# One tile at a time in the first pass of a two-layer decoder trunk: work order on four engines, and a share of the weight splitting moved to GpSimd

## The chip, the core and the metric

The kernel runs on one core of one Trainium2 chip. Its engines are named as the profile names them: PE (TensorE, matrix products; PEld is its weight loads), DVE (VectorE), ACT (ScalarE), POOL (GpSimd) and SP (SyncE, which here only issues DMA transfers). Each engine works through its own queue in order and waits on semaphores for the others. The metric is the device time of one execution in microseconds (us), median of several runs.

## The reference

Two decoder layers over 256 tokens of width 1024. Each layer is a token mixer (dilated window attention in layer 0, gated linear attention in layer 1) and a gated feed-forward part. Ahead of each, the tokens are normed and then scaled and shifted by vectors that come from a conditioning vector c:

```python
mod = jax.nn.silu(c) @ w_ada[i] + b_ada[i]
sh1, sc1, g1, sh2, sc2, g2 = jnp.split(mod, 6, axis=-1)
h = rmsnorm(x, norm_mix[i]) * (1.0 + sc1) + sh1
y = dilated_mixture(h, w_in_a[j], w_out_a[j], rel_bias)   # begins with qkv = h @ w_in_a[j]
```

This case is about the first product of layer 0 only: h @ w_in_a for the first heads, for which sc1 and sh1 have to be computed first. Everything is float32.

## The kernel before

**Three products for one.** A float32 product is made of rounded parts: a weight tile is cast to a reduced format ("whi"), and the rest is kept beside it ("wlo", raw less whi). The normed tokens have the same two parts, hhi and hlo. PE then does hhi with whi (part 0), hlo with whi (part 1) and hhi with wlo (part 2).

**The first pass** runs over eight tiles kt of 128 rows of the model's width. Each needs two transfers on SP's queue: `ada_raw` (or `early_x`, a borrowed room), 128 x 2048 columns of w_ada, of which the second half gives sc1 and the first half sh1, and `raw`, 1920 columns of w_in_a. For tiles 0 and 1 each transfer is cut in two. The 1920 columns are two halves in the code's words, `pieces`: columns 0 to 768 (half 0) and 768 to 1920 (half 1). The work of one tile is:

- `dots` (L421, L160): on DVE two products of 1024 columns with silu(c), each summed to one column; behind each, ACT makes the entry of `mod`, at L168 the scale, at L170 the shift.
- `scaled` (L430): xr on DVE, the tokens times rstd and the scale.
- `shifted` (L434): hhi on ACT, xr plus the shift, cast.
- `rest_of` (L438): hlo on DVE, xr plus the shift less hhi.
- `cast` (L446): whi of one half, on ACT, 768 or 1152 columns.
- `low` (L451): wlo of one half, on DVE.
- `products` (L683): on PE one part for some of three pieces. Piece 0 (six matmuls of 256 columns, from half 0) and piece 2 (six, from the last 768 columns of half 1) are queries and keys of two head pairs; piece 1 (two matmuls of 384 columns, L690, from the first 384 columns of half 1) is the values.

**What sets the order.** A scheduler places the instructions, but `behind` (L120) ties each to one that stands ahead of it on the same engine, and so the order on DVE, ACT and PE in this pass is the one written out. From tile 2 on it is shifted by a tile: ACT casts both halves of tile kt-1 and then makes the two `mod` entries and hhi of tile kt; DVE does the dots of kt, low half 0 of kt-1, xr of kt, low half 1 of kt-1, hlo of kt. On PE a tile's part 2 stands in among the parts 0 and 1 of the next one. GpSimd has no part in it; it copies the bias table (L368) up to 18.9 us and issues bias transfers (L382, L383) from 47.9 us.

**Buffers.** `raw` and `ada_raw` share four buffers, so a transfer of a later tile is issued when the dots or the lows of an earlier one are done with theirs. whi and wlo have three buffers each. Behind the pass come the evacuation of its results from PSUM (L601 to L609), the casts and lows of the next weights (L189, L193) and the next matmuls (L658).

Of the kernel before, what the change touches and what calls it, by code (L numbers as in the profile page):

```python
# [11 lines left out]
F32 = mybir.dt.float32  # L12
# [3 lines left out]
AF = mybir.ActivationFunctionType  # L16
ALU = mybir.AluOpType

P = 128
D = 1024  # L20
T = 256
KT = D // P
# [18 lines left out]
C_NMIX = C_BADA + 96  # L41
C_NFFN = C_NMIX + 16
# [15 lines left out]
def trunk(ctx: ExitStack, tc: tile.TileContext, I, out):  # L58
    nc = tc.nc
# [12 lines left out]
    def bank(name="ps", tag=None):  # L72
        tag = tag or next(cycle)
        return psum.tile([P, 512], F32, tag=tag, name=name, bufs={"p": 2, "s": 4, "t": 2}[tag])
# [21 lines left out]
    def col(at):  # L96
        return small[:, at : at + 1]
# [11 lines left out]
    one_b = const.tile([P, 32], F32, name="one_b")  # L109

    def scale_terms(sub):
        at = C_BADA + 24 * sub + 8
        b = small[:, at : at + 96].rearrange("p (l k) -> p l k", l=2)[:, :, 0:KT]
        g = small[:, (C_NMIX, C_NFFN)[sub] :][:, 0:16].rearrange("p (l k) -> p l k", l=2)
        return nc.vector.scalar_tensor_tensor(one_b[:, 16 * sub : 16 * sub + 16].rearrange("p (l k) -> p l k", l=2), b, 1.0, g,
                                              op0=ALU.add, op1=ALU.mult)


    @contextmanager
    def behind(*those):  # L120

        with ExitStack() as st:
            for i in those:
                st.enter_context(tc.issue_after(i.ins))
            yield
# [27 lines left out]
        return modulation(raw, l, n)  # L153

    def modulation(raw, l, n, order=(0, 1), between=None):
        for s in order:
            piece, kt = ADA_ORDER[2 * n + s]
            dot = tmp.tile([P, 1], F32, tag="dot", name="dot", bufs=4)
            w = raw[:, D * s : D * s + D]
            last_dot[0] = nc.vector.tensor_tensor_reduce(  # L160
                w, w, c_bc, op0=ALU.mult, op1=ALU.add, scale=1.0, scalar=0.0, accum_out=dot,
            )
            m = state.tile([P, 1], F32, tag=f"mod{l}{piece}{kt}", name="mod")
            b = col(C_BADA + 48 * l + 8 * piece + kt)
            if piece in (1, 4):
                g = col((C_NMIX if piece == 1 else C_NFFN) + 8 * l + kt)
                b1 = (16 if piece == 4 else 0) + 8 * l + kt
                last = nc.scalar.activation(m, dot, AF.Identity, scale=g, bias=one_b[:, b1 : b1 + 1])  # L168
            else:
                last = nc.scalar.activation(m, dot, AF.Identity, bias=b)  # L170
            mod[l, piece, kt] = m
            if between and s == order[0]:
                between(last)
        return last


# [227 lines left out]
    w0, h, xr, raw0 = [], [], [None] * KT, []  # L404
    pieces = (slice(0, 6 * P), slice(6 * P, 15 * P))
    on_act = [norm_ops[1]]
# [2 lines left out]

    def load(kt):  # L410
        chunk = rooms[0] if kt % 2 else wraw.tile([P, 2048], F32, tag="raw", name="ada_raw")
        for c in (slice(D, 2 * D), slice(0, D)) if kt < 2 else (slice(0, 2 * D),):
            nc.sync.dma_start(chunk[:, c], I["w_ada"][0, kt][:, c])
        raw = wraw.tile([P, 2048], F32, tag="raw", name="raw")
        for c in pieces if kt < 2 else (slice(0, 15 * P),):
            last_load[0] = nc.sync.dma_start(raw[:, c], I["w0"][kt][:, c])
        raw0.append(raw)
        w0.append([wspl.tile([P, 2048], F32R, tag=f"w{part}", name=f"w{part}") for part in ("hi", "lo")])
        return chunk

    def dots(kt, between=None):  # L421
        chunk = load(kt)
        with behind(on_dve[0], on_act[0]):
            on_act[0] = modulation(chunk, 0, kt, (1, 0), between)
        on_dve[0] = last_dot[0]

    def scaled(kt):
        xr[kt] = tmp.tile([P, T], F32, tag="xr", name="xr")
        with behind(on_dve[0]):
            on_dve[0] = nc.vector.scalar_tensor_tensor(xr[kt], x[kt], mod[0, 1, kt][:, 0:1], r, op0=ALU.mult, op1=ALU.mult)  # L430

    def shifted(kt):
        with behind(on_act[0]):
            on_act[0] = nc.scalar.activation(h_hi[kt][:, :], xr[kt], AF.Identity, bias=mod[0, 0, kt][:, 0:1])  # L434

    def rest_of(kt):
        with behind(on_dve[0]):
            on_dve[0] = nc.vector.scalar_tensor_tensor(h_lo[kt][:, :], xr[kt], mod[0, 0, kt][:, 0:1], h_hi[kt][:, :].bitcast(F32),  # L438
                                                       op0=ALU.add, op1=ALU.subtract)
        chain[kt] = chain[7] = on_act[0], on_dve[0]  # L440
        h.append((h_hi[kt], h_lo[kt]))

    def cast(kt, half):
        c = pieces[half]
        with behind(on_act[0]):
            on_act[0] = nc.scalar.copy(w0[kt][0][:, c], raw0[kt][:, c])  # L446

    def low(kt, half):
        c = pieces[half]
        with behind(on_dve[0]):  # L450
            on_dve[0] = nc.vector.tensor_tensor(w0[kt][1][:, c], raw0[kt][:, c], w0[kt][0][:, c].bitcast(F32), op=ALU.subtract)  # L451

    def first_cast(last):
        on_act[0] = last
        cast(0, 0)

    dots(0, first_cast)
    scaled(0)
    shifted(0)
    low(0, 0)  # L460
    rest_of(0)
    cast(0, 1)
    dots(1)
    scaled(1)
    low(0, 1)
    shifted(1)
    rest_of(1)
    for kt in range(2, KT):
        for half in range(2):
            cast(kt - 1, half)  # L470
        dots(kt)
        low(kt - 1, 0)
        scaled(kt)
        low(kt - 1, 1)
        shifted(kt)
        rest_of(kt)
    for half in range(2):
        cast(KT - 1, half)
    for half in range(2):
        low(KT - 1, half)  # L480
    scale_terms(1)
    with tc.issue_after(last_load[0].ins):
        nc.sync.dma_start(rows_d, rows)
# [84 lines left out]
    def turn(tiles, normed_p, pt):  # L568
        for i in tiles:
            t = bank("t", "ttss"[i])  # L570
            for j in range(3):
                c = slice(P * j, P * j + P)
                last = nc.tensor.transpose(t[:, c], normed_p[i][:, c], ident)
            pt_copy[0] = nc.scalar.copy(pt[:, i, :], t[:, 0:KEYS])
        return last
# [103 lines left out]
    b1 = [bank("pqk", tg) for tg in "sss"]  # L679
    pqk1 = [b[:, T * i : T * i + T] for b in b1 for i in range(2)]  # L680
    last = [warm]

    def products(kt, part, pieces):  # L683
        w, y = w0[kt][part == 2], h[kt][part == 1]
        s, e = part == kt == 0, part == 2 and kt == KT - 1
        with behind(*last):
            for piece in pieces:
                if piece == 1:
                    for t in range(2):
                        i = mm(pv[t][:, : NG * P], y[:, P * t : P * t + P], w[:, 6 * P : 9 * P], start=s, stop=e)  # L690
                    continue
                at, ps = ((0, pqk0), None, (9 * P, pqk1))[piece]
                for j in ((2, 3, 4, 5, 0, 1), (), range(6))[piece]:
                    i = mm(ps[j], w[:, at + P * j : at + P * j + P], y, start=s and j % 2 == 0, stop=e and j % 2 == 1)  # L694
        last[0] = i

    for piece in (0, 2, 1):
        for part in range(3 if piece == 0 else 2):
            products(0, part, (piece,))
    for kt in range(1, KT):  # L700
        products(kt - 1, 2, (0,) if kt > 1 else (2, 1))
        products(kt, 0, range(3))
        if kt > 1:
            products(kt - 1, 2, (1, 2))
        products(kt, 1, range(3))
    products(KT - 1, 2, (0,))
    products(KT - 1, 2, (1, 2))

    qk0, qk1 = new_qk(), new_qk()
    left = [evacuate(*qk, g, pqk[2 * g], pqk[2 * g + 1])  # L710
# [4 lines left out]
    bias = load_bias(0)  # L715
# [3 lines left out]
    with behind(end):  # L719
        s, last = scores(*qk0)  # L720
# [12 lines left out]
    with behind(end):  # L733
        s, last = scores(*qk1)
    raised = maxima(s, bias1)

    for u in range(2, NPAIR):
        if u > 2:
            bias = load_bias(u)
# [5 lines left out]
        if u == 2:  # L745
            bias = load_bias(u)
# [4 lines left out]
        first = pt_copy[:1] if u == 2 else ()  # L751
# [14 lines left out]
        with behind(end, turned):  # L766
            s, last = scores(*qk)
        with behind(last):
            last = outputs(u - 1, v, before[1])
# [6 lines left out]
    def between(n, kt):  # L776
        if (n, kt) == (0, 3):
            turn((0, 1), *before)
        elif (n, kt) == (0, 6):
            turn((2, 3), *before)  # L780
        elif (n, kt) == (1, 3):
            outputs(NPAIR - 1, v, before[1])
# [251 lines left out]
    for n in range(4):  # L1034
# [7 lines left out]
        for i in range(2):  # L1042
            kt = 2 * n + i
            for t in range(2):
                ht = [y[:, P * t : P * t + P] for y in h[kt]]
                for s in range(2):
                    with behind(*last_gate if kt == 5 else ()):
                        last = mm3(pv[t][s], ht, parts(w, D * i + 512 * s, 512), kt == 0, kt == KT - 1)
# [303 lines left out]
    with behind(last_pd[0]):  # L1352
        last = mean_square([0])
    with behind(last):
        last = turned(range(2))
    with behind(last):
        last = mean_square([1])
# [7 lines left out]
    for half in range(2):  # L1365
        for t, own in enumerate(halves):
            c = slice(512 * half, 512 * half + 512)
# [118 lines left out]
```

## Time and profile before

| what | value |
|---|---|
| median of 3 runs | 757.47 us (756.81 to 757.93) |
| the profiled execution | 757.76 us |
| its span | 755.9 us |
| PE busy | 747.5 us (99%) |
| DVE busy | 629.7 us (83%) |
| ACT busy | 490.0 us (65%) |
| POOL busy | 73.1 us (10%) |
| granted PE clock, mean | 0.998 |

The span runs from the first to the last instruction of the program; the execution's time has 1.86 us beside it. A row of a timeline gives the start and the duration in us, the engine, the line, the operation, what is written from what, the shapes and the count of merged instructions; in brackets stands the idle time before it and what ended it. A row of busy times by stretch gives for each engine the busy time and in brackets the instructions, then the granted clock, the DMA engines' share and GB/s.

### The profile page before, as it was taken

Reading aid. Unit: us, or ns where it says so; the run is one execution under the profiler, and the core shown is the slowest. Engines: PE = TensorE matmul, PEld = TensorE weight load, DVE = VectorE, ACT = ScalarE, POOL = GpSimd, SP = SyncE. Lnnn points to the kernel's source line nnn. Section 1 sums busy time; section 2 is a strip of 40 time slices with the busy share of each in tenths; the row PEclk is TensorE's granted clock in tenths of the full one; section 3 lists DMA queues with packets and bytes.
Section 4 is the critical chain, followed back from the end, with each engine's and each line's share of the span. In section 5 each row is a group of like instructions: output and inputs, shape, how many; then the busy total and the mean of one; then the engine's idle time right before and its main releaser. Section 6 shows DMA issues by size and latency. Waiting matters only on the chain.

```text
span 755.9 us, 15967 instructions
## 1 busy us (share of the span) xinstructions
PE 747.5 (99%) x6410; PEld 727.5 (96%) x6410; DVE 629.7 (83%) x1120; ACT 490.0 (65%) x954; POOL 73.1 (10%) x148
## 2 busy tenths in 40 slices
PE   9999999999999999999999999999999999999997
PEld 7899999999999999999999998999999999999996
DVE  6988978887888688999988778986897989898662
ACT  6466677566675588776766457844878766666552
POOL 6033320220200010000000002000010000000100
PEclk9999999999999999999999999999999999999999
DMA  9999789887886666766656985864475756656641
GB/s 344 417 348 362 243 300 312 292 277 290 281 286 232 216 223 231 277 239 227 219 179 226 325 308 190 330 252 136 145 279 171 276 180 211 196 181 218 246 165 56
DMA packets 31420, 186.83 MB, mean 247 GB/s; under 512 B 4321, under 2 KB 4705, under 8 KB 15218
## 3 DMA queue, kind: packets, MB, share of 16 engines
q1 hardware_dynamic: 26240, 162.38, 60.3%
q0 software_dynamic: 4784, 23.09, 9.5%
q8 instruction: 50, 0.82, 0.4%
q10 hardware_dynamic: 322, 0.35, 0.1%
q14 instruction: 24, 0.20, 0.1%
HBM read 184.70 MB, written 1.10 MB: 246 GB/s over the span
## 4 chain that ended last, share of the span: by engine, by line
PE 91%; DVE 3%; DMA 3%; ACT 1%; issue 1%; SPq 0%; DVEq 0%; ACTq 0%
PE pab L216 10%; PE pab L215 10%; PE pab L214 10%; PE pd L214 5%; PE pd L216 5%; PE pd L215 5%; PE pqk L214 5%; PE pqk L216 4%; PE pqk L215 4%; PE pv L215 3%; PE pv L216 3%; PE pv L214 3%; PE pqk L694 3%; DMA early_x<-in_w_ada 2%; PE py L215 2%; PE py L216 2%
## 5 line engine op out<-in xcount | busy, mean ns | idle before, releaser
L193 DVE TENSOR_TENSOR wlo<-raw,whi 128x1024 fp32r<-128x1024 f32 (+3 forms) x254 | 272.0, 1102 | 53.1 <-ACT whi L189 52.2
L189 ACT CAST whi<-raw 128x1024 fp32r<-128x1024 f32 (+3 forms) x254 | 228.2, 947 | 107.3 <-PE pab L215 41.9
L216 PE MATMUL pab<-hhi,wlo 128*128 128x256 f32 x672 | 185.1, 277 | 0.0
L215 PE MATMUL pab<-hlo,whi 128*128 128x256 f32 x672 | 185.0, 277 | 0.0
L214 PE MATMUL pab<-hhi,whi 128*128 128x256 f32 x672 | 183.5, 277 | 0.0
L216 PEld LDWEIGHTS pab<-hhi,wlo 128*128 128x128 f32 x672 | 126.3, 188 | 0.0
L215 PEld LDWEIGHTS pab<-hlo,whi 128*128 128x128 f32 x672 | 126.1, 188 | 0.2
L214 PEld LDWEIGHTS pab<-hhi,whi 128*128 128x128 f32 x672 | 125.3, 188 | 0.1
L216 PE MATMUL pd<-ghi,wlo 128*128 128x256 f32 x352 | 97.1, 276 | 0.0
L215 PE MATMUL pd<-glo,whi 128*128 128x256 f32 x352 | 97.1, 276 | 0.0
L214 PE MATMUL pd<-ghi,whi 128*128 128x256 f32 x352 | 96.8, 276 | 0.0
L214 PE MATMUL pqk<-hhi,whi 128*128 128x256 f32 x314 | 88.0, 280 | 0.0
L216 PE MATMUL pqk<-hhi,wlo 128*128 128x256 f32 x314 | 86.8, 276 | 0.0
L215 PE MATMUL pqk<-hlo,whi 128*128 128x256 f32 x314 | 86.8, 276 | 0.0
L160 DVE CUSTOM_DVE_ANT_0 ada_raw<-ada_raw,c_bc 128x1024 f32<-128x1024 f32 x52 | 61.3, 1219 | 11.4 <-DMA ada_raw<-in_w_ada 11.4
L215 PEld LDWEIGHTS pd<-glo,whi 128*128 128x128 f32 x352 | 66.1, 188 | 0.0
L216 PEld LDWEIGHTS pd<-ghi,wlo 128*128 128x128 f32 x352 | 66.1, 188 | 0.0
L214 PEld LDWEIGHTS pd<-ghi,whi 128*128 128x128 f32 x352 | 65.9, 188 | 0.0
L214 PEld LDWEIGHTS pqk<-hhi,whi 128*128 128x128 f32 x314 | 59.0, 188 | 0.4
L215 PEld LDWEIGHTS pqk<-hlo,whi 128*128 128x128 f32 x314 | 59.0, 188 | 0.0
L216 PEld LDWEIGHTS pqk<-hhi,wlo 128*128 128x128 f32 x314 | 59.0, 188 | 0.0
L895 ACT ACTIVATE r<-pab,small 128x256 f32<-128x256 f32 x86 | 46.6, 558 | 15.5 <-DVE r L898 15.4
(244 smaller groups left out, 1502.0 us busy)
## 6 DMA issues: line engine op xcount, KB each, us to landing
raw<-in_w_up SPq DMA_DIRECT2D x42, 1024.0 KB, 4.9
ada_raw<-in_w_ada SPq DMA_DIRECT2D x25, 1024.0 KB, 5.3
raw<-in_w_down SPq DMA_DIRECT2D x32, 704.0 KB, 4.3
raw<-in_wqk SPq DMA_DIRECT2D x18, 1024.0 KB, 6.2
raw<-in_wv SPq DMA_DIRECT2D x14, 768.0 KB, 6.2
early_x<-in_w_ada POOLq DMA_DIRECT2D x9, 1024.0 KB, 7.3
x_all<-in_w_ada POOLq DMA_DIRECT2D x9, 1024.0 KB, 5.8
raw<-in_w SPq DMA_DIRECT2D x6, 960.0 KB, 7.6
```

The lines of the kernel that those rows point to most:

```text
L160: last_dot[0] = nc.vector.tensor_tensor_reduce(w, w, c_bc, op0=ALU.mult, op1=ALU.add, scale=1.0, scalar=0.0, accum_out=dot,)
L189: copied[0] = nc.scalar.copy(hi[:, c], raw[:, c])
L193: last_lo[0] = nc.vector.tensor_tensor(lo[:, c], raw[:, c], hi[:, c].bitcast(F32), op=ALU.subtract)
L214: mm(ps, a[0], b[0], start=start, stop=False)
L215: mm(ps, a[0], b[1], start=False, stop=False)
L216: return mm(ps, a[1], b[0], start=False, stop=stop)
L694: i = mm(ps[j], w[:, at + P * j : at + P * j + P], y, start=s and j % 2 == 0, stop=e and j % 2 == 1)
L895: nc.scalar.activation(r, u[:, :T], AF.Identity, scale=cw[2], bias=col(C_CB + 44 * l + f))
```

## The change

Five sets of edits, all in the first pass:

- ACT: the cast of half 0 of the same tile now stands between the two `mod` operations of each tile (before, only in tile 0), tied there by `first`; the cast of half 1 stands behind hhi.
- DVE: dots, xr, low half 0, hlo, low half 1 of one tile, then the next tile. In tile 1 the order is dots, xr, low half 1 of tile 0, hlo, both lows of tile 1.
- GpSimd: from tile 2 on the last 384 columns of low half 1 are computed there; DVE does the other 768.
- PE: no part of a tile is left to the next one, except in tile 0. From tile 2 on: part 0 of pieces 0 and 2, part 1 of the same, values part 0, part 2 of piece 0, values parts 1 and 2, part 2 of piece 2.
- SP: the transfers of tiles 2 and 3 are cut in two as those of tiles 0 and 1 are.

```diff
     def modulation(raw, l, n, order=(0, 1), between=None):
+        first = ()
         for s in order:
...
-            if piece in (1, 4):
...
+            with behind(*first):
+                if piece in (1, 4):
...
             if between and s == order[0]:
-                between(last)
+                first = between(last)
...
-        for c in (slice(D, 2 * D), slice(0, D)) if kt < 2 else (slice(0, 2 * D),):
+        for c in (slice(D, 2 * D), slice(0, D)) if kt < 4 else (slice(0, 2 * D),):
...
-        for c in pieces if kt < 2 else (slice(0, 15 * P),):
+        for c in pieces if kt < 4 else (slice(0, 15 * P),):
...
     def low(kt, half):
         c = pieces[half]
+        if half and kt > 1:
+            own = slice(c.stop - 3 * P, c.stop)
+            nc.gpsimd.tensor_tensor(w0[kt][1][:, own], raw0[kt][:, own], w0[kt][0][:, own].bitcast(F32), op=ALU.subtract)
+            c = slice(c.start, own.start)
...
-    for kt in range(2, KT):
-        for half in range(2):
-            cast(kt - 1, half)
-        dots(kt)
-        low(kt - 1, 0)
-        scaled(kt)
-        low(kt - 1, 1)
-        shifted(kt)
-        rest_of(kt)
...
+    def tile_of(kt):
+        def first_cast(last):
+            on_act[0] = last
+            cast(kt, 0)
+            return on_act[:1]
+
+        dots(kt, first_cast)
         scaled(kt)
         shifted(kt)
+        cast(kt, 1)
+
+    for kt in range(KT):
+        tile_of(kt)
+        if kt != 1:
+            low(kt, 0)
+            rest_of(kt)
+        if kt == 1:
+            low(0, 1)
+            rest_of(1)
+            low(1, 0)
+        if kt:
+            low(kt, 1)
...
+    for part in range(3):
+        products(0, part, (0,))
+    for part in range(2):
+        products(0, part, (2,))
+    products(0, 0, (1,))
+    products(1, 0, (0,))
+    for part in (1, 2):
+        products(0, part, (1,))
+    products(0, 2, (2,))
     for kt in range(1, KT):
-        products(kt - 1, 2, (0,) if kt > 1 else (2, 1))
-        products(kt, 0, range(3))
-        if kt > 1:
-            products(kt - 1, 2, (1, 2))
-        products(kt, 1, range(3))
...
+        products(kt, 0, (0, 2) if kt > 1 else (2,))
+        products(kt, 1, (0, 2))
+        products(kt, 0, (1,))
+        products(kt, 2, (0,))
+        for part in (1, 2):
+            products(kt, part, (1,))
+        products(kt, 2, (2,))
```

More of the change, by code (lines that the diff above doesn't have):

```diff
@@ L164, in modulation @@
             b = col(C_BADA + 48 * l + 8 * piece + kt)
-            if piece in (1, 4):
[L166 to L170, printed above, removed]
+            with behind(*first):
+                if piece in (1, 4):
+                    g = col((C_NMIX if piece == 1 else C_NFFN) + 8 * l + kt)
+                    b1 = (16 if piece == 4 else 0) + 8 * l + kt
+                    last = nc.scalar.activation(m, dot, AF.Identity, scale=g, bias=one_b[:, b1 : b1 + 1])
+                else:
+                    last = nc.scalar.activation(m, dot, AF.Identity, bias=b)
             mod[l, piece, kt] = m
             if between and s == order[0]:
-                between(last)
+                first = between(last)
         return last
@@ L449, in low @@
         c = pieces[half]
+        if half and kt > 1:
+            own = slice(c.stop - 3 * P, c.stop)
+            nc.gpsimd.tensor_tensor(w0[kt][1][:, own], raw0[kt][:, own], w0[kt][0][:, own].bitcast(F32), op=ALU.subtract)
+            c = slice(c.start, own.start)
         with behind(on_dve[0]):
             on_dve[0] = nc.vector.tensor_tensor(w0[kt][1][:, c], raw0[kt][:, c], w0[kt][0][:, c].bitcast(F32), op=ALU.subtract)
[L453 to L467, printed above, removed]
-    for kt in range(2, KT):
-        for half in range(2):
-            cast(kt - 1, half)
-        dots(kt)
-        low(kt - 1, 0)
+    def tile_of(kt):
[4 more added lines that the diff above has]
+        dots(kt, first_cast)
         scaled(kt)
-        low(kt - 1, 1)
         shifted(kt)
-        rest_of(kt)
[L477 to L480, printed above, removed]
+        cast(kt, 1)
[10 more added lines that the diff above has]
+            low(kt, 1)
     scale_terms(1)
@@ L695, in products @@
         last[0] = i
-    for piece in (0, 2, 1):
-        for part in range(3 if piece == 0 else 2):
-            products(0, part, (piece,))
-    for kt in range(1, KT):
-        products(kt - 1, 2, (0,) if kt > 1 else (2, 1))
-        products(kt, 0, range(3))
-        if kt > 1:
-            products(kt - 1, 2, (1, 2))
-        products(kt, 1, range(3))
-    products(KT - 1, 2, (0,))
-    products(KT - 1, 2, (1, 2))
+    for part in range(3):
[7 more added lines that the diff above has]
+    products(0, 2, (2,))
+    for kt in range(1, KT):
+        products(kt, 0, (0, 2) if kt > 1 else (2,))
[5 more added lines that the diff above has]
+        products(kt, 2, (2,))
     qk0, qk1 = new_qk(), new_qk()
```

## The prediction

> **What bounds the kernel now.** I read the head of the page first, then the busy times by stretch, the waits of two engines, and the timelines of the first pass.
>
> ```profile
> span 755.9 us, 15967 instructions
> PE 747.5 (99%) x6410; PEld 727.5 (96%) x6410; DVE 629.7 (83%) x1120; ACT 490.0 (65%) x954; POOL 73.1 (10%) x148
> ```
> ```profile
> 13.13:32.00 18.87, 17.29 (x129) 15.97 (x128) 16.55 (x27) 9.57 (x16) 5.78 (x15) 1.00 1.02 418
> 32.00:58.50 26.50, 26.50 (x212) 26.50 (x210) 22.85 (x36) 16.49 (x29) 8.77 (x16) 1.00 0.97 367
> ```
> Over the whole span PE idles 8.4 us, so a shift of PE in the first pass is a shift of the end. The pass runs from 13.1 to 58.6 us. All of PE's idle time in it lies before 32 us (17.29 busy of 18.87); behind that PE is never idle (26.50 of 26.50). The last three columns are the granted clock, the DMA share and GB/s: the DMA engines are full up to 32 us at 418 GB/s.
>
> ```profile
> 19.57 1.23 DVE L160 CUSTOM_DVE_ANT_0 ada_raw<-ada_raw,c_bc 128x1024 f32<-128x1024 f32 x1 [1.59 <-DMA ada_raw<-in_w_ada]
> 25.58 1.22 DVE L160 CUSTOM_DVE_ANT_0 early_x<-early_x,c_bc 128x1024 f32<-128x1024 f32 x1 [0.69 <-DMA early_x<-in_w_ada]
> ...
> 30.81 1.22 DVE L160 CUSTOM_DVE_ANT_0 ada_raw<-ada_raw,c_bc 128x1024 f32<-128x1024 f32 x1
> ...
> 31.95 1.21 DVE L160 CUSTOM_DVE_ANT_0 ada_raw<-ada_raw,c_bc 128x1024 f32<-128x1024 f32 x1
> 33.10 0.95 DVE L451 TENSOR_TENSOR wlo<-raw,whi 128x768 fp32r<-128x768 f32 x1
> 33.97 0.47 DVE L430 SCALAR_TENSOR_TENSOR xr<-x_all,mod,rstd 128x256 f32<-128x256 f32 x1
> 34.37 1.35 DVE L451 TENSOR_TENSOR wlo<-raw,whi 128x1152 fp32r<-128x1152 f32 x1
> 35.64 0.47 DVE L438 SCALAR_TENSOR_TENSOR hlo<-xr,mod,hhi 128x256 fp32r<-128x256 f32 x1
> 36.03 1.21 DVE L160 CUSTOM_DVE_ANT_0 early_x<-early_x,c_bc 128x1024 f32<-128x1024 f32 x1
> ```
> The two bracketed rows are the only times that DVE waits for data, for tiles 2 and 3. From 25.58 on it works without a gap, one tile per 5.22 us (30.81 to 36.03). Start to start: dots 1.14 and 1.15, low half 0.87, xr 0.40, low rest 1.27, hlo 0.39; the ends overlap the next start by 0.08.
>
> ```profile
> 23.73 1.87 ACT L446 CAST whi<-raw 128x768 fp32r<-128x768 f32 x2
> 24.60 0.97 PE L694 MATMUL pqk<-hhi,whi 128*128 128x256 f32 x6 [0.75 <-ACT whi L446]
> ...
> 57.56 0.51 PE L690 MATMUL pqk<-wlo,hhi 128*128 128x384 f32 x2
> 57.91 0.87 PE L694 MATMUL pqk<-hhi,wlo 128*128 128x256 f32 x6
> 58.62 2.05 PE L658 MATMUL pqk<-hhi,whi 128*128 128x256 f32 x16
> ```
> On PE a block of six matmuls takes 0.71 (57.91 to 58.62), a pair for the values 0.35. A tile has six and three: 5.31 us, 42.5 for eight. So PE and DVE are nearly even a tile, and the pass, whose first matmul starts at 13.15 (a row further down), loses 58.62 - 13.15 - 42.5 = 3.0 us, all to the late start of tiles 1 to 3.
>
> **The change part by part.** *What it removes.* Low weights of tile 1 now stand behind tile 2's dots, which wait for data to 19.57; after, they fill that wait. DVE is through with tile 1's hlo near 17.9:
>
> ```profile
> 16.24 1.35 DVE L451 TENSOR_TENSOR wlo<-raw,whi 128x1152 fp32r<-128x1152 f32 x1
> 17.50 0.48 DVE L438 SCALAR_TENSOR_TENSOR hlo<-xr,mod,hhi 128x256 fp32r<-128x256 f32 x1
> ```
> ```profile
> 16.41 0.51 ACT L434 ACTIVATE hhi<-xr,mod 128x256 fp32r<-128x256 f32 x1 [0.17 <-DVE xr L430]
> 16.83 1.88 ACT L446 CAST whi<-raw 128x768 fp32r<-128x768 f32 x2
> ```
> ACT does the same things in another order and is through by 18.71 (16.83 + 1.88) at the latest; a cast ahead of hhi delays it by at most 0.8, of which DVE's chain covers about 0.5. Then low 0.87 from 17.9 and low rest 1.27: tile 2's dots start at 20.05, 0.5 later than now, but with nothing owed. Call a tile's start of dots t; t(2) = 20.05. PE is then busy to 13.15 + 2 x 5.31 = 23.8, and 0.3 more for tile 1's hhi; tile 2's hhi is ready at t + 3.4 = 23.5 (next part). So PE starts tile 2 at 24.1 without a wait, where it now starts at 24.60 (above) with blocks of tile 1 still owed, and ends it at 29.4.
>
> *A tile in one go.* The order on DVE is dots, xr, low half, hlo, low rest. Dots 2.29, xr to 2.69, low half to 3.56, hlo to 3.95. The next needs the second cast, which ACT reaches late:
>
> ```profile
> 34.54 0.51 ACT L434 ACTIVATE hhi<-xr,mod 128x256 fp32r<-128x256 f32 x1 [1.03 <-DVE xr L430]
> 34.95 0.82 ACT L446 CAST whi<-raw 128x768 fp32r<-128x768 f32 x1
> 35.68 1.16 ACT L446 CAST whi<-raw 128x1152 fp32r<-128x1152 f32 x1
> ```
> Xr ends at t + 2.76, hhi begins 0.10 later (34.44 to 34.54) and ends at 3.37, the cast of 1152 columns begins 0.10 before that and ends at 4.43. The first cast (0.82) fits between the two short mod operations. So DVE stands still from 3.95 to 4.46: this wait is new, 0.5 us a tile; behind it in DVE's queue are the low rest and all dots of the next tile. Before, low work of the tile ahead filled it.
>
> *GpSimd's 384 columns.* DVE's low rest falls from 1152 to 768 columns, 1.27 to 0.87, so it frees DVE at t + 5.33. What GpSimd's operation costs DVE no row shows at this size. The nearest are an addition of 256 columns and a subtraction of 512 on 16 partitions:
>
> ```profile
> 413.98 0.80 POOL L246 TENSOR_TENSOR sqacc<-sq 128x256 f32<-128x256 f32 x1 [143.81 <-ACT sq L243]
> ...
> 460.15 1.35 POOL L965 TENSOR_TENSOR w_g<-w_gate,w_g 16x512 fp32r<-16x512 f32 x1
> ```
> ```profile
> 411.30 1.68 DVE L193 TENSOR_TENSOR wlo<-raw,whi 128x704 fp32r<-128x704 f32 x2
> ...
> 414.10 1.43 DVE L193 TENSOR_TENSOR wlo<-raw,whi 128x704 fp32r<-128x704 f32 x1
> ...
> 460.27 1.51 DVE L296 SCALAR_TENSOR_TENSOR hlo<-xr,mod,hhi 128x256 fp32r<-128x256 f32 x1
> ```
> A low of 704 columns takes 0.88 (two in 1.68, with the overlap); with GpSimd adding 256 columns at that moment it takes 1.43, that is 0.55 more. An hlo (0.47 in the DVE rows above) takes 1.51 beside 512 columns: 1.04 more. So GpSimd and DVE take turns, at 2.03 to 2.15 ns a column. For 384 columns: 0.78 to 0.83, and I take **0.80**. Bounds: 0, if the subtraction runs beside DVE; 1.10, 1.5 times GpSimd's own span when little stands in its way:
>
> ```profile
> 269.43 0.73 POOL L246 TENSOR_TENSOR sqacc<-sqacc,sq 128x256 f32<-128x256 f32 x1
> ```
> The Trainium skill (SBUF — State Buffer, "Who interferes with whom") speaks against this edit: a DVE instruction with two SBUF inputs shuts out a GpSimd instruction that reads SBUF, and the later one waits until the first has finished. By the whole instruction the price would be the 1.10 and not the 0.80; the rows say that DVE is let in earlier (0.55 of a span of 0.80).
>
> Both wait for the same cast, so whoever starts first, DVE loses 0.80 and saves 0.40. A tile then takes 5.33 + 0.80 = **6.13 us** against 5.22 now.
>
> *The sum.* t(7) = 20.05 + 5 x 6.13 = 50.70. On PE the last tile starts at t + 3.41; its second block waits for the second cast and starts at 4.47; a block behind a wait takes 0.79 (13.15 to 13.94):
>
> ```profile
> 13.15 0.94 PE L694 MATMUL pqk<-hhi,whi 128*128 128x256 f32 x6
> 13.94 0.84 PE L694 MATMUL pqk<-hlo,whi 128*128 128x256 f32 x6
> ```
> so 5.26, 5.97, 6.68, then values 7.03, block 7.74, values 8.09 and 8.44, last block 9.15. The pass ends at 59.85 against 58.62: **+1.2 us**. PE's loss in the pass is 4.2 us in place of 3.0: next to nothing to 29 us, then 0.8 a tile from tile 3 on. Nothing behind the pass gives it back, since PE is full there.
>
> *Edits at nothing.* Six blocks in another order on PE are the same blocks. Splitting the loads of tiles 2 and 3 adds four issues on SP, whose queue waits for buffers anyway; a half that lands earlier saves nothing, as t(2) hangs on DVE (20.05, data at 19.57) and t(3) too (26.2, data at 25.55). Later tiles need 1024 and 960 KB, 2.03 MB, each:
>
> ```profile
> ada_raw<-in_w_ada SPq DMA_DIRECT2D x25, 1024.0 KB, 5.3
> ...
> raw<-in_w SPq DMA_DIRECT2D x6, 960.0 KB, 7.6
> ```
> That is 4.9 us at 418 GB/s, under the 6.13. Were DVE at 5.33, this cover would be thin (0.4 us) but still there.
>
> The profiled execution took 757.76 us, 1.86 beside its span and 0.29 over the median of 757.47. So I forecast 758.96 against that execution, **758.7** against the median. What a measurement here can tell from no change is about 0.2%, 1.5 us.
>
> **Rivals.**
> *GpSimd runs beside DVE (faster).* Price 0: a tile takes 5.33. t(3) = 25.5, t(7) = 46.8, PE is the bound again, and the pass ends near 56.0: -2.6, 754.9. For it: the rows above are of additions and of sixteen partitions, none is this shape. Against it: both DVE operations there were stretched. The two cases meet at no change for a price of 0.55: (58.62 - 9.15 - 20.05) / 5 - 5.33.
> *DVE blocked for the whole GpSimd span.* 1.10: a tile takes 6.43, t(7) = 52.2, the pass ends at 61.35: +2.7, 760.2. Against it: the 0.55 above. By the rule of the Trainium skill above, taken by its letter, it would be this one.
> *Casts of the next stage in ACT's queue (slower).* The next stage's casts stand behind the last cast of the pass now:
>
> ```profile
> 51.67 1.15 ACT L446 CAST whi<-raw 128x1152 fp32r<-128x1152 f32 x1
> 52.73 1.04 ACT L189 CAST whi<-raw 128x1024 fp32r<-128x1024 f32 x1
> ```
> With the buffers free earlier in a tile's order, one may be queued ahead of tile 7's hhi or second cast. It decides when those weights are in SBUF before t(7) + 2.8: 0.95 on the last tile's chain, +2.1, 759.6. Against it: the casts now wait for their turn.
> *GpSimd's part comes late, so the change does not do what it says.* Its queue also issues the bias transfers:
>
> ```profile
> 47.91 0.69 POOL L382 DMA_DIRECT2D bias<-rows_d  x1 [28.99 <-DMA rows_d<-rows]
> 51.89 0.62 POOL L383 DMA_DIRECT2D bias<-rows_d  x1
> ```
> If tile 6's or 7's part stands behind them, PE's last block waits to about 53.5 instead of 53.0: +0.5 to +1.0, 759.2 to 759.7. The queue's other waits come later.
>
> **How the numbers follow.** Forecast 0.55, beside DVE 0.20, whole span 0.08, casts 0.10, late 0.07. The forecast's own range is 757.9 to 759.6 (price 0.65 to 0.95). The range of 754.9 to 760.4 takes in the bounds on both sides. Over 1.5 us faster: the first rival and a little of the forecast, 0.21. Slower by as much: 0.4 of the forecast, nearly all of the other three, 0.39. Within: 0.40.
>
> **What would show it.** DVE's tile period in the first pass about 6.1 us, with 0.4 to 0.5 idle ahead of the 768-column low of the second half, ended by ACT's cast; in each tile from the third on one DVE operation 0.8 longer than its like, next to a GpSimd row that writes wlo; PE idle about 0.8 a tile in tiles 3 to 7 and not before 29 us; DMA well under 418 GB/s from 32 us. Wrong it is if DVE's dots keep 1.2 us beside GpSimd's rows, if the period is under 5.9, or if PE's idle stands ahead of its last blocks.

## The result: 7.0 us slower, and the profile after

The changed kernel takes 764.34 us (764.01 to 764.91) against 757.34 (756.81 to 757.93): ratio 1.0091, interval 1.0078 to 1.0104. The forecast was 758.7 and the range ended at 760.4, so both missed. The profiled execution took 764.05 us.

The page of the changed kernel, its head and first busy times, and three stretches (columns as before: busy time of PE, PEld, DVE, ACT, POOL, then granted clock, DMA share, GB/s):

```profile
span 762.2 us, 15987 instructions
...
PE 750.3 (98%) x6410; PEld 728.8 (96%) x6410; DVE 630.5 (83%) x1120; ACT 490.1 (64%) x954; POOL 87.1 (11%) x154
```
```profile
54.00:57.40 3.40, 0.17 (x3) 0.01 (x1) 1.51 (x3) 2.85 (x4) 2.18 (x4) 0.93 0.47 83
57.40:60.00 2.60, 2.60 (x12) 2.60 (x13) 0.00 (x0) 1.54 (x2) 2.58 (x5) 0.50 0.60 181
...
56.90:60.30 3.40, 2.90 (x13) 2.91 (x14) 0.00 (x0) 1.56 (x2) 3.38 (x6) 0.50 0.58 169
```
Up to 54 us PE keeps the pace of the forecast. Then PE stands still for 3.2 us, and when it goes on its granted clock is 0.50, from 56.9 to 60.3.

The timeline of PE in the changed kernel, around that place; the brackets give the idle time before a row and what ended it:

```profile
53.65 0.51 PE L694 MATMUL pqk<-hhi,wlo 128*128 128x256 f32 x3
57.40 1.01 PE L694 MATMUL pqk<-hhi,wlo 128*128 128x256 f32 x3 [3.23 <-POOL wlo L454]
58.20 2.53 PE L694 MATMUL pqk<-hhi,whi 128*128 128x256 f32 x12
60.57 1.58 PE L694 MATMUL pqk<-hlo,whi 128*128 128x256 f32 x12
...
64.44 2.05 PE L658 MATMUL pqk<-hhi,whi 128*128 128x256 f32 x16
```
The first three matmuls of tile 6's last block need DVE's columns of wlo and run at 53.65. The other three need GpSimd's columns and wait to 57.40. The next twelve take 2.37 us (58.20 to 60.57), the twelve after them 1.41. The pass ends at 64.44 instead of 58.62: 5.8 of the 6.3 us by which the span is longer are there already.

Why GpSimd is late shows its own timeline:

```profile
43.59 1.74 POOL L454 TENSOR_TENSOR wlo<-raw,whi 128x384 fp32r<-128x384 f32 x1 [4.41 <-ACT whi L448]
45.48 0.69 POOL L384 DMA_DIRECT2D bias<-rows_d  x1 [0.16 <-issue]
...
51.13 0.52 POOL L384 DMA_DIRECT2D bias<-rows_d  x1 [1.05 <-DMA bias<-rows_d]
...
54.73 0.52 POOL L384 DMA_DIRECT2D bias<-rows_d  x1 [1.40 <-DMA bias<-rows_d]
55.72 0.59 POOL L385 DMA_DIRECT2D bias<-rows_d  x1 [0.47 <-DMA bias<-rows_d]
56.33 1.01 POOL L454 TENSOR_TENSOR wlo<-raw,whi 128x384 fp32r<-128x384 f32 x1
...
59.51 1.02 POOL L454 TENSOR_TENSOR wlo<-raw,whi 128x384 fp32r<-128x384 f32 x1
```
The shares of tiles 2 to 5 run as soon as ACT has cast their columns. The share of tile 6 comes at 56.33, though its cast ended at 49.61 (48.47 + 1.14 in the ACT row below): fourteen issues of bias transfers stand ahead of it in GpSimd's queue, and three of them wait for earlier bias transfers to land (1.05, 1.40 and 0.47 us).

```profile
48.47 1.14 ACT L448 CAST whi<-raw 128x1152 fp32r<-128x1152 f32 x1
```

The part of the forecast that concerned DVE came out almost to the digit. DVE's timeline in the changed kernel:

```profile
31.18 0.96 DVE L457 TENSOR_TENSOR wlo<-raw,whi 128x768 fp32r<-128x768 f32 x1 [0.42 <-ACT whi L448]
32.06 2.04 DVE L161 CUSTOM_DVE_ANT_0 ada_raw<-ada_raw,c_bc 128x1024 f32<-128x1024 f32 x1
34.03 1.21 DVE L161 CUSTOM_DVE_ANT_0 ada_raw<-ada_raw,c_bc 128x1024 f32<-128x1024 f32 x1
...
37.34 0.96 DVE L457 TENSOR_TENSOR wlo<-raw,whi 128x768 fp32r<-128x768 f32 x1 [0.42 <-ACT whi L448]
38.21 2.04 DVE L161 CUSTOM_DVE_ANT_0 early_x<-early_x,c_bc 128x1024 f32<-128x1024 f32 x1
...
50.52 1.22 DVE L161 CUSTOM_DVE_ANT_0 early_x<-early_x,c_bc 128x1024 f32<-128x1024 f32 x1
```
A tile takes 6.15 us (32.06 to 38.21; forecast 6.13). The low rest waits 0.42 us for ACT's cast, and the first dots behind a share take 2.04 instead of 1.22, 0.82 more (taken: 0.80). At 50.52 the dots take 1.22 again, because tile 6's share was not there to take its turn.

### The profile page after: what moved, and what is told of

It reads as the page before. It is cut to its first block, busy times and chain, and to the rows that moved or that the text cites. A ratio compares the mean times of both kernels' runs of the same rounds, so it can differ in the third digit from the quotient of the medians.

```text
span 762.2 us, 15987 instructions
## 1 busy us (share of the span) xinstructions
PE 750.3 (98%) x6410; PEld 728.8 (96%) x6410; DVE 630.5 (83%) x1120; ACT 490.1 (64%) x954; POOL 87.1 (11%) x154
## 4 chain that ended last, share of the span: by engine, by line
PE 84%; DVE 6%; DMA 4%; ACT 2%; issue 2%; POOL 1%; SPq 0%; ACTq 0%; DVEq 0%; POOLq 0%
PE pab L217 10%; PE pab L216 10%; PE pab L218 10%; PE pd L217 5%; PE pd L218 5%; PE pd L216 5%; PE pqk L216 5%; PE pqk L218 4%; PE pqk L217 4%; PE pv L217 3%; PE pv L218 3%; PE pv L216 2%; PE py L217 2%; PE py L218 2%; PE py L216 2%
## 5 line engine op out<-in xcount | busy, mean ns | idle before, releaser
L161 DVE CUSTOM_DVE_ANT_0 ada_raw<-ada_raw,c_bc 128x1024 f32<-128x1024 f32 x52 | 63.0, 1252 | 10.7 <-DMA ada_raw<-in_w_ada 10.7
```

What stands on the lines that cost most here:

```text
L161: last_dot[0] = nc.vector.tensor_tensor_reduce(w, w, c_bc, op0=ALU.mult, op1=ALU.add, scale=1.0, scalar=0.0, accum_out=dot,)
```

## The experiments

In each, times are compared with the kernel before on the same chip.

### The place in GpSimd's queue

The changed kernel with one order added: the bias transfers of the first head pair stand behind the share of tile 6, the room loads and the bias transfers of the second pair behind that of tile 7. `on_pool` keeps the instruction of each share.

```diff
+    on_pool = {}
...
-            nc.gpsimd.tensor_tensor(w0[kt][1][:, own], raw0[kt][:, own], w0[kt][0][:, own].bitcast(F32), op=ALU.subtract)
+            on_pool[kt] = nc.gpsimd.tensor_tensor(w0[kt][1][:, own], raw0[kt][:, own], w0[kt][0][:, own].bitcast(F32), op=ALU.subtract)
...
-    bias = load_bias(0)
-    with behind(last_bias[0]):
+    with behind(on_pool[KT - 2]):
+        bias = load_bias(0)
+    with behind(last_bias[0], on_pool[KT - 1]):
...
-    bias1 = load_bias(1)
+    with behind(on_pool[KT - 1]):
+        bias1 = load_bias(1)
```

> The changed kernel with one order added on GpSimd's queue: the bias transfers of the first head pair behind GpSimd's share of tile 6, those of the second and the room loads behind its share of tile 7. Theory (the loss is the place in the queue): the share of tile 6 runs within 1 us of its cast, PE's wait of 3.2 us goes, the granted clock stays at 1.00, and the pass ends where the port alone puts it, t(7) = 20.6 + 5 x 6.15 = 51.3, plus 9.15: 60.5 instead of 64.4. Time 759.2 to 760.3. Rival (GpSimd is kept from the data by DVE, whatever stands ahead of it in its queue): the wait of PE stays and the time with it, 763 to 764.5.

Measured: 758.86 us (757.68 to 760.25) against 757.08, ratio 1.0023 (1.0013 to 1.0032). GpSimd's and PE's timelines in this kernel:

```profile
48.92 1.73 POOL L455 TENSOR_TENSOR wlo<-raw,whi 128x384 fp32r<-128x384 f32 x1 [4.41 <-ACT whi L449]
50.60 0.69 POOL L384 DMA_DIRECT2D bias<-rows_d  x1
...
55.19 1.62 POOL L455 TENSOR_TENSOR wlo<-raw,whi 128x384 fp32r<-128x384 f32 x1
```
```profile
53.95 2.02 PE L695 MATMUL pqk<-hhi,whi 128*128 128x256 f32 x12 [0.36 <-ACT hhi L437]
55.80 1.52 PE L695 MATMUL pqk<-hlo,whi 128*128 128x256 f32 x12
...
59.59 1.98 PE L659 MATMUL pqk<-hhi,whi 128*128 128x256 f32 x16
```
The share of tile 6 runs at 48.92, PE waits for nothing of GpSimd's, the clock stays at 1.00 in the pass, and it ends at 59.59, 4.85 us earlier. The theory of the queue holds, and the rival falls: GpSimd gets its turn against DVE whenever its queue lets it. In ratios 0.68% of the 0.91% are the queue's, about 5.1 us; the other 0.23%, 1.7 us, are what the forecast was about. By the two intervals the 5.1 are uncertain by about 1.2 us. Of the 4.85 us in the two traces 0.79 are an earlier start: DVE reaches the dots of tile 2 at 19.78 in this execution and at 20.57 in that of the changed kernel. So some 4.1 us of the pass are the queue's.

### Shares in tiles 2 to 5 only

```diff
-        if half and kt > 1:
+        if half and 1 < kt < KT - 2:
```

> The changed kernel with GpSimd's share in tiles 2 to 5 only; DVE does all of tiles 6 and 7, and the bias transfers keep the place they have in the changed kernel. Theory (only the shares that stand behind bias transfers cost the 5.5 us): no wait of PE for GpSimd, clock 1.00, t(7) = 20.0 + 4 x 6.15 + 5.73 = 50.3, pass end 59.5, time 758.0 (757.4 to 758.8). Rival (the early bias transfers themselves, or the buffers held by GpSimd, make the loss): 761 or more.

Measured: 758.29 us (757.96 to 758.66) against 757.33, ratio 1.0009 (0.9999 to 1.0018). Here the bias transfers keep their early place and do no harm, with nothing behind them that PE needs. So it is the two shares behind them, and not the transfers, that cost the 5 us.

### The port: no share, and half a share

"The port" is short here and below for what the prediction read out of its rows: GpSimd and DVE take turns, and a turn of GpSimd's costs DVE time.

No share at all, DVE does the 1152 columns (the rest as changed):

```diff
-        if half and kt > 1:
+        if False:
```

> The changed kernel without GpSimd's share: DVE does all 1152 columns of the low rest. Theory (the port's price is 0.8 us a tile, of which 0.4 net): a tile takes 5.33 + 0.40 = 5.73 us on DVE instead of 6.15, no DVE operation is stretched, t(7) = 20.6 + 5 x 5.73 = 49.2, the pass ends at 58.4, where it ends before (58.6). Time 757.1 (756.4 to 758.0). Rival (the order of one tile in one go is itself what costs, the port little): 759 or more.

Measured: 756.71 us (756.15 to 757.37) against 757.08, ratio 0.9994 (0.9985 to 1.0003): no difference from the kernel before that can be told. Its DVE rows:

```profile
29.95 1.36 DVE L457 TENSOR_TENSOR wlo<-raw,whi 128x1152 fp32r<-128x1152 f32 x1 [0.42 <-ACT whi L448]
31.23 1.22 DVE L161 CUSTOM_DVE_ANT_0 ada_raw<-ada_raw,c_bc 128x1024 f32<-128x1024 f32 x1
...
35.68 1.36 DVE L457 TENSOR_TENSOR wlo<-raw,whi 128x1152 fp32r<-128x1152 f32 x1 [0.42 <-ACT whi L448]
```
A tile takes 5.73 (29.95 to 35.68), the expected figure, and no dots are stretched; the wait for the cast stays. So moving work to GpSimd made DVE slower, 6.15 against 5.73.

A share of 192 columns, with the bias transfers behind the shares:

```diff
-            own = slice(c.stop - 3 * P, c.stop)
+            own = slice(c.stop - 3 * P // 2, c.stop)
```

> The changed kernel with the bias transfers behind GpSimd's shares, and a share of 192 columns instead of 384. Theory (DVE is shut out for the time that GpSimd reads, about 2 ns a column, with little that is fixed): the dots that follow a share are 0.40 to 0.45 us longer (0.82 with 384 columns), DVE's low of 960 columns is 0.20 longer, a tile takes 5.33 + 0.20 + 0.42 = 5.95 us against 6.15, the pass ends about 1.0 earlier than with 384 columns; time 757.6 to 758.4. Rival (each turn costs a fixed amount, whatever the size): dots longer by 0.7 to 0.8, a tile of 6.3 us, time 759 or more.

Measured: 757.55 us (757.03 to 758.56) against 757.33, ratio 1.0003 (0.9994 to 1.0013). The dots behind a share:

```profile
30.55 1.16 DVE L458 TENSOR_TENSOR wlo<-raw,whi 128x960 fp32r<-128x960 f32 x1 [0.42 <-ACT whi L449]
31.63 1.62 DVE L161 CUSTOM_DVE_ANT_0 ada_raw<-ada_raw,c_bc 128x1024 f32<-128x1024 f32 x1
...
36.49 1.16 DVE L458 TENSOR_TENSOR wlo<-raw,whi 128x960 fp32r<-128x960 f32 x1 [0.42 <-ACT whi L449]
```
They take 1.62, which is 0.40 more than 1.22, and a tile takes 5.94. Half the columns, half the price: 2.1 ns a column, nothing fixed that shows. DVE itself needs 1.05 ns for a column (1.36 less 1.16 us for 192), so each column given away costs DVE twice what it saves.

### The share alone, in the order of before

The kernel before with the share, and with the bias transfers behind the shares by the edits shown above:

```diff
     def low(kt, half):
         c = pieces[half]
+        if half and kt > 1:
+            own = slice(c.stop - 3 * P, c.stop)
+            on_pool[kt] = nc.gpsimd.tensor_tensor(...)
+            c = slice(c.start, own.start)
```

> The kernel before, in its own order on DVE, ACT, PE and SP, with GpSimd's share of 384 columns from tile 2 on alone, and the bias transfers behind it in the queue. Theory (the port): each share stretches one DVE operation by 0.8, a tile takes 5.22 - 0.40 + 0.82 = 5.64 us on DVE where it takes 5.22; the kernel's slack of about 1.2 us between hhi of tile 7 and its first use on PE takes up most of the 4 x 0.42; the pass ends 0.4 to 0.7 later, time 757.4 to 758.2. Rival (the share is harmless in that order): no stretched operation, a tile of 4.8 us, time 756.3 to 757.2.

Measured: 761.32 us (760.78 to 762.05) against 757.33, ratio 1.0050 (1.0035 to 1.0065), more than expected. DVE rows and PE's waits of this kernel (who waited for whom: us in total, times, longest):

```profile
33.41 1.76 DVE L456 TENSOR_TENSOR wlo<-raw,whi 128x768 fp32r<-128x768 f32 x1
...
39.04 1.76 DVE L456 TENSOR_TENSOR wlo<-raw,whi 128x768 fp32r<-128x768 f32 x1
```
```profile
PE pqk L699 <- ACT whi L447: 1.5, 2, 0.8
PE pv L215 <- DVE wlo L193: 1.3, 2, 1.1
```
The port acts as expected: the low behind a share takes 1.76 instead of 0.95, and a tile 5.63 us (33.41 to 39.04; expected 5.64). What was wrong is the slack behind it. In this order the casts of a tile stand on ACT behind that tile's hhi, which waits for DVE's xr, and PE waits for these casts; so it follows DVE's pace. The next stage begins at 60.62 (58.62 before), with three matmuls of the pass still to come. Another 1.3 us go in the next stage, where PE waits for the low weights of the values. The share is bad in either order.

### PE's standstill and the clock

The changed kernel with PE kept busy ahead of tile 6's last block. The added matmuls multiply ones into columns that nothing reads.

```diff
+        if kt == KT - 2:
+            with behind(*last):
+                for _ in range(9):
+                    last[0] = mm(pv[0][:, 3 * P : 4 * P], ones_d, ones_d, start=False, stop=False)
         products(kt, 2, (2,))
```

> The changed kernel with nine matmuls of no use (ones by ones, into columns that nothing reads) ahead of PE's last block of tile 6, so that PE is busy while it waits for GpSimd. Theory (the granted clock fell to 0.50 because PE stood still for 3.2 us): the clock stays at 1.00 through the last tile, which takes 5.4 instead of 6.2 us; the wait itself stays, and the last block of tile 6 runs whole behind it (0.35 more): pass end 63.7 to 64.0, time 763.4 to 764.0. Rival (the slow start of the last tile has another cause than the standstill): clock as before, time 764.5 to 764.9.

Measured: 764.74 us (763.4 to 766.2) against 757.08, ratio 1.0103 (1.0089 to 1.0116). Two stretches, PE's timeline and its waits:

```profile
54.00:57.40 3.40, 1.92 (x17) 1.72 (x16) 0.96 (x1) 2.67 (x4) 3.19 (x6) 1.00 0.26 55
57.40:60.00 2.60, 2.60 (x25) 2.60 (x24) 0.00 (x0) 1.02 (x2) 2.58 (x4) 1.00 0.86 230
```
```profile
56.87 0.62 PE L694 MATMUL pqk<-hhi,wlo 128*128 128x256 f32 x3 [1.48 <-POOL wlo L454]
57.33 1.53 PE L694 MATMUL pqk<-hhi,whi 128*128 128x256 f32 x12
...
62.49 1.98 PE L658 MATMUL pqk<-hhi,whi 128*128 128x256 f32 x16
...
74.92 0.44 PE L217 MATMUL pv<-wlo,hhi 128*128 128x384 f32 x1 [0.57 <-DVE wlo L195]
...
81.66 0.38 PE L216 MATMUL pqk<-hhi,whi 128*128 128x256 f32 x1 [1.13 <-ACT v L619]
```
On the clock the theory holds: it stays at 1.00, and the last tile takes 5.16 us (57.33 to 62.49) where it took 6.24. The Trainium skill (TensorE: Matmul & The Clock Gate, "Part 1: The HAM clock gate") puts this in a rule: about 3.4 us of an idle PE, in windows that run freely, halve its clock, and as long a time of work restores it. The changed kernel's trace agrees on the length of the slow stretch, 3.4 us, and not on the idle time:

```profile
53.50:56.90 3.40, 0.66 (x5) 0.45 (x3) 2.01 (x3) 3.33 (x4) 1.68 (x3) 1.00 0.60 105
56.80:56.90 0.10, 0.00 (x0) 0.00 (x0) 0.00 (x0) 0.03 (x1) 0.10 (x1) 1.00 0.01 0
56.90:57.00 0.10, 0.00 (x0) 0.00 (x0) 0.00 (x0) 0.00 (x0) 0.10 (x1) 0.52 0.00 0
```
The clock falls at 56.9, 2.7 us after PE's last matmul has ended (53.65 + 0.51 = 54.16), and in the 3.4 us before it falls PE is still busy for 0.66. With a standstill of 1.5 us, in the run with the added matmuls, it does not fall; where between 1.5 and 2.7 us the limit lies, and whether it depends on the moment, no run here shows.

On the time the expectation was wrong: it did not get better that one could tell (1.0103 against 1.0091, with intervals that overlap). PE is through with the pass 1.95 us earlier. Of these 0.53 come from a share that ends earlier in this execution (56.87 against 57.40), and 1.4 from the clock: 0.34 in the three matmuls behind the wait, 1.08 in the last tile. PE then loses 1.7 us in the next stage, in waits that the changed kernel does not have: 0.57 at 74.92 for low weights of the values, and 1.13 at 81.66. The span is 0.7 us shorter (761.5 against 762.2), in what was the fastest of four executions.

The loads of that stage are late in both kernels. The second transfer of the values' weights is issued on SP's queue only when GpSimd's share of tile 6 has let go of its buffer. The issues in the changed kernel (the second of the two is at 47.59 + 10.11 less its own 0.33, so at 57.37), what SP's queue waited for GpSimd's low weights there from 45 to 60 us, and the issues before:

```profile
47.59 10.11 SPq L185 DMA_DIRECT2D raw<-in_wv  x2
```
```profile
SPq L185 <- POOL wlo L454: 7.6, 2, 6.7
```
```profile
46.22 5.55 SPq L183 DMA_DIRECT2D raw<-in_wv  x2
```
In the kernel before it is issued at 51.45, in the run with the added matmuls at 56.84. So the late share holds up two things, PE and the loads of the next stage. That PE's two waits at 74.92 and 81.66 go back to these late loads is likely and not shown: no run here frees the buffer early and leaves the share late.

### An order without either loss

Without the share, with the low rest of a tile done one tile later, so that DVE has work while ACT casts; PE takes the parts that need it behind the next tile's first block. Below this order is called skewed.

```diff
-        if half and kt > 1:
+        if False:
...
     for kt in range(KT):
         tile_of(kt)
+        if kt:
+            low(kt - 1, 1)
         if kt != 1:
             low(kt, 0)
-            rest_of(kt)
+        rest_of(kt)
         if kt == 1:
-            low(0, 1)
-            rest_of(1)
-            low(1, 0)
-        if kt:
-            low(kt, 1)
+            low(kt, 0)
+    low(KT - 1, 1)
...
-        products(kt, 0, (0, 2) if kt > 1 else (2,))
+        if kt > 1:
+            products(kt, 0, (0,))
+            for piece in (1, 2):
+                products(kt - 1, 2, (piece,))
+        products(kt, 0, (2,))
         products(kt, 1, (0, 2))
         products(kt, 0, (1,))
         products(kt, 2, (0,))
-        for part in (1, 2):
-            products(kt, part, (1,))
-        products(kt, 2, (2,))
+        products(kt, 1, (1,))
+    for piece in (1, 2):
+        products(KT - 1, 2, (piece,))
```

> The changed kernel without GpSimd's share and with the low rest of a tile on DVE one tile later: dots, xr, low rest of the tile before, low half, hlo; on PE the parts that need it stand behind the next tile's first block. Theory (the two losses of one tile in one go are DVE's 0.5 us wait for the second cast and the port): no wait is left on DVE but for data, a tile takes 5.22 us there, PE is the bound from tile 2 on and ends at about 13.3 + 0.4 + 42.5 = 56.2. Time 754.9 (754.3 to 756.0). Rival (data come too late for PE in tiles 3 and 4, as they do before): 756.5 to 757.5.

Measured: 754.66 us (754.34 to 755.64) against 757.08, ratio 0.9969 (0.9957 to 0.9981). The pass in this kernel by stretch, and its last row on PE:

```profile
14.25:56.97 42.72, 42.68 (x339) 42.36 (x338) 39.08 (x61) 26.12 (x45) 16.82 (x23) 1.00 1.00 389
```
```profile
56.97 2.05 PE L657 MATMUL pqk<-hhi,whi 128*128 128x256 f32 x16
```
PE is busy for 42.68 of 42.72 us: in this execution the pass has nothing left to lose once it has begun. It begins at 14.25, though, 1.1 us later than before, and ends at 56.97 where 56.2 was expected. In the second execution of the same kernel, further down, it begins at 13.52, PE waits 0.7 us in it, and it ends at 57.00. The kernel is faster than both others and its time is the expected one; the theory of the two losses stands.

### Whole transfers for tiles 2 and 3

Undoing the split of the loads, once in the changed order with the bias transfers behind, once in the skewed order; then the skewed pair again on one chip.

```diff
-... if kt < 4 else ...
+... if kt < 2 else ...      # both lines of load()
```

> The changed kernel with the bias transfers behind GpSimd's shares, and with the transfers of tiles 2 and 3 whole, as before. Theory (in this order the halves are worth nothing, since DVE reaches the dots of tile 2 at 19.8 or later and those of tile 3 at 25.9 with the share ahead of them, behind the whole transfers at 19.6 and 25.6): as with the halves, 758.9 (758.2 to 759.4). Rival (they are worth about 1 us, as the first comparison of the skewed order suggests): 759.5 to 760.5.

> The faster order (low rest of a tile one tile later, no GpSimd share) with the transfers of tiles 2 and 3 whole again, as before. Theory (splitting them is worth nothing, as DVE's chain or the total of the transfers sets tiles 2 and 3): 754.7 (754.2 to 755.6), no wait of PE in the pass. Rival (the halves are what brings tile 2 early): tile 2's dots start at 19.5 or later instead of 19.3 and tile 3's at 25.6 instead of 24.5, PE waits 0.3 to 1.0: 755.2 to 756.0.

> The skewed order with halves once more, unchanged, beside the others on one chip. If the halves are worth what the two runs suggest (754.7 with, 756.1 without), 754.7 again (754.3 to 755.2). If the difference lay in the runs: 755.4 to 756.1.

> The skewed order with whole transfers once more, unchanged, beside the others on one chip. If the halves are worth about 1.4 us: 756.1 (755.8 to 756.6). If the difference lay in the runs: 754.7 to 755.4.

Measured, as ratios to the kernel before (it took 758.16 on the chip of the last comparison):

| order | halves | whole |
|---|---|---|
| changed, bias behind | 1.0023 (1.0013 to 1.0032) | 1.0021 (1.0013 to 1.0030), 759.60 us |
| skewed | 0.9969 (0.9957 to 0.9981) | 0.9980 (0.9970 to 0.9990), 756.09 us |
| skewed, same chip | 0.9963 (0.9949 to 0.9976), 755.62 us | 0.9977 (0.9967 to 0.9988), 756.11 us |

The expected times can't be held against the measured ones of the last three runs, since the kernel before took 1.1 us longer on the last chip than on the first; the ratios can. In the changed order the halves are worth nothing: 1.0021 of the first chip's 757.08 is 758.7, the theory's time, though the 759.60 as measured lies in the rival's range. In the skewed order they come out better twice, by 0.11 and 0.14%, about 0.8 to 1.1 us, with intervals that overlap. The traces show 0.3 us of it: the pass ends at 56.97 and 57.00 with halves, and at 57.28 twice without, where the dots of tile 3 start at 25.66 and 25.65 instead of 24.50 and 24.52. So it is likely a gain, and its size is not settled.

## Why the prediction was wrong

- **The step that failed is the fourth rival**, "GpSimd's part comes late". It was named, and sized at +0.5 to +1.0 with a chance of 0.07. It decided the case, at about +5.1. The mis-sized term has three parts. "The queue's other waits come later" was false: the issues wait for earlier bias transfers, 2.9 us in sum, and fourteen of them stand ahead of the share. PE's last block waited to 57.4, not 53.5. And the price stopped at PE's wait: the clock at 0.50 behind it (about 1.4 us of PE time) and the buffer that SP's queue waits for were left out. The prediction's own last sign of being wrong, idle time of PE ahead of its last blocks, is what came.
- **The place in the queue.** The two GpSimd edits were priced by what they do to DVE. Nothing tied the shares to a place in GpSimd's queue, and the scheduler put two of them behind issues that wait; the share of tile 6, ready at 49.61, stood there to 56.33. The rows that show the bias issues from 47.9 us were quoted, and the shares of tiles 6 and 7 were due at 49 and 55; the bias transfers also began 2.4 us earlier than before (45.48 against 47.91), which the prediction did not look for. The transfer that they need, rows_d, is issued on SP's queue at 39.58, and at 41.38 before.
- **The port was right**: 0.80 taken, 0.82 measured; a tile 6.13 against 6.15; the wait for the second cast 0.5 against 0.42. With the bias transfers behind the shares the pass ends at 59.59, where the sum said 59.85, and the kernel is 1.7 us slower than before (1.0 to 2.4), where the sum said 1.2. That its 758.86 stands so near to the 758.7 is in part luck, since the kernel before took 757.08 there and not 757.47.
- **"GpSimd runs beside DVE" was wrong**: each of the four dots that a share met in the changed kernel took 2.04 instead of 1.22. **"Blocked for the whole span" had the size wrong**: the spans are 1.74 to 1.79 us beside DVE and 1.01 alone, and DVE loses 0.82, not 1.10.
- **Casts of the next stage in ACT's queue** did not happen: they stand behind the second cast of tile 7.
- **Edits at nothing.** For the split of the loads that was right in this order. **The early part** was right: PE waits 0.38 us up to 29 us. The dots of tile 2 started at 20.57 instead of 20.05; in the five other runs with this order and the halves they started at 19.77 to 20.16.
- **"Nothing behind the pass gives it back"** was right; more is lost behind it (the span is 6.3 us longer, the pass 5.8).
- **The chances** do not add up by their own words: 0.4 of the forecast's 0.55 and nearly all of the other three's 0.25 are about 0.46 for slower, not 0.39, and leave 0.33 for no change.

## What to carry to other kernels

An operation that is moved to another engine is also moved into that engine's queue: list what stands ahead of it there at each of its due times and what those instructions wait for, and give it a place by hand if nothing else does. Price a column on GpSimd by what it takes from DVE when both read two operands, here 2.1 ns against 1.05 saved. And when the consumer is late, look one step further: at the buffers that the late operation holds, and at the clock if PE would stand still for longer than the 1.5 us that left it alone here.

## What the runs showed of the hardware that was not expected

One standstill of PE of 3.2 us brought the granted clock to 0.50 for 3.4 us; it fell 2.7 us into the standstill, while PE was still idle. A standstill of 1.5 us, and the waits of 0.25 to 0.4 us between tiles, left it at 1.00. The price of a GpSimd turn to DVE went straight with its columns, 0.40 us for 192 and 0.82 for 384.
